# The feed-forward layers' first product by Strassen's seven block products, and their second product in four phases

## The chip, the cores and the metric

The kernel runs on one core of a Trainium2 chip. The metric is the time of one execution on the device, in microseconds; less is better.

## What is computed

A two-layer encoder on 512 tokens of width 1024, in float32. Each layer has a half-step SwiGLU feed-forward (FFN), a mixer of three token-mixing groups, and a second half-step FFN, so there are four FFNs. Around each sub-layer stand an RMS norm, a shift and scale, and a gate, which come from the conditioning vector c by a matrix product (adaLN). What matters here, from the reference:

```python
def swiglu(h, w_in, w_out):
    gate, up = jnp.split(h @ w_in, 2, axis=-1)
    return (jax.nn.silu(gate) * up) @ w_out
...
        h = modulate(rms_norm(x), sh1, sc1)
        x = x + 0.5 * g1[:, None, :] * swiglu(h, w_ff1_in[l], w_ff1_out[l])
```

w_in is 1024 x 5632 and w_out 2816 x 1024: in tiles of 128, w_in gives 22 tiles of gate columns and 22 of up columns, each with 8 tiles along the 1024 rows.

## The kernel before, in words

Activations lie feature by token: a tile is 128 features by 512 tokens. Each product is made of three float32r matmuls (`mm3`, L213 to L220): every float32 operand is split into a high part, a rounded copy by ScalarE (ACT), and a low part, the difference by VectorE (DVE) (`split`, L162 to L165). So the weights of one tile column, 128x1024, go by DMA into a `raw` tile (three buffers), by a cast into `wh` and by a subtraction into `wl` (two buffers each), in `weights` (L167 to L174).

`ffn` (L464 on) runs in two halves of 11 column pairs. For a pair j the gate product `pg` and the up product `pu` are 8 x 3 matmuls of 512 tokens each, so 48 per pair; then ScalarE takes SiLU of `pg`, VectorE multiplies by `pu` (L489), and the result is split into `ah` and `al`. After 11 pairs the second product runs: for each of 8 output tiles m, 33 matmuls into `po`, and VectorE adds gate times `po` to the residual x (`update_x`, L398). In the second half the last two output tiles are done in `tail`, in two token halves of 256 columns, so that the next norm can start on the first half.

The first FFN of layer 0 gets its first four pairs from `start` (L432 on), which streams the normed input row tile by row tile into eight PSUM banks (`pst`). The other FFNs take their first one or two pairs in `norm_first`, beside the norm.

The adaLN product is background work: `ada` (L294 to L301) loads a 128x1024 piece of its matrix and reduces it on VectorE in one instruction. There are 144 pieces; `bg_step` is called after each weight load in an FFN and issues one piece (or a piece of the rotary tables). GpSimd (POOL) adds two shifted copies in the mixer (`shift`, L707) and is idle in the FFNs.

The order on each engine is made by the framework's scheduler from the program's order and its priorities; the kernel's own means are the buffer counts of its pools and where `bg_step` stands. In names below, PE is TensorE and SP the queue that issues the DMAs.

Of the kernel before, what the change touches and what calls it, by code (L numbers as in the profile page):

```python
# [1508 lines left out]
```

## Time and profile before

| what | value |
|---|---|
| median of 3 runs | 2333.05 us (2330.82 to 2336.97) |
| span of the profiled execution | 2329.9 us |
| TensorE (PE) busy | 97% of the span |
| VectorE (DVE) busy | 56% |
| ScalarE (ACT) busy | 40% |
| GpSimd (POOL) busy | 1% |
| mean granted TensorE clock | 0.995 |

The span runs from the first to the last instruction of one profiled execution; the page gives no other time for that execution, and the median of the runs lies 3.1 us above its span. Busy PE time is read with care, because the ends of matmuls are modelled and they overlap: the distance from one start to the next is what a matmul costs.

### The profile page before, as it was taken

To read this page: it belongs to the slowest core of one execution; us is meant where nothing else is said; L and a number is where in the kernel's file an instruction comes from. 1 tells how busy PE (TensorE), PEld (TensorE's weight loads), DVE (VectorE), ACT (ScalarE), POOL (GpSimd) and SP (SyncE) were. 2 spreads that over 40 slices of the span, in tenths; PEclk is the share of its full clock that TensorE was granted. 3 is DMA by queue.
4 is the path that set the end of the run, shared out by engine and by line. 5 is a ranking of instruction groups with operands and counts; after the bars stand their busy time and mean duration, and the time that the engine had idled before them with its cause. 6 is when DMAs were issued, how large, how long until landed. Compare 5 with 4: busy or idle time off the path is not lost.

```text
span 2329.9 us, 33848 instructions
## 1 busy us (share of the span) xinstructions
PE 2269.9 (97%) x14006; PEld 1804.1 (77%) x14006; DVE 1299.0 (56%) x2113; ACT 932.1 (40%) x1473; POOL 32.2 (1%) x48
## 2 busy tenths in 40 slices
PE   6999999999999999999999999999999999999998
PEld 5888888677655788888888888887776568888887
DVE  7656865469555754333455655445785566333334
ACT  3322344533656533223433223454445564322232
POOL 0000000200000000000000000011000000000000
PEclk9999999999999999999999999999999999999999
DMA  7555553212100343332435665322220012223322
GB/s 294 195 204 189 189 200 105 73 55 73 36 18 8 125 153 138 108 100 91 144 110 195 214 219 193 115 73 73 63 57 24 10 35 89 84 90 107 97 89 86
DMA packets 83770, 263.45 MB, mean 113 GB/s; under 512 B 10272, under 2 KB 13600, under 8 KB 83616
## 3 DMA queue, kind: packets, MB, share of 16 engines
q1 hardware_dynamic: 82896, 259.69, 33.7%
q8 instruction: 109, 1.79, 0.3%
q10 hardware_dynamic: 720, 1.61, 0.2%
q14 instruction: 45, 0.37, 0.0%
HBM read 257.07 MB, written 2.10 MB: 111 GB/s over the span
## 4 chain that ended last, share of the span: by engine, by line
PE 88%; DVE 6%; ACT 3%; DMA 2%; issue 1%; POOL 0%; SPq 0%; DVEq 0%; ACTq 0%
PE po L218 7%; PE po L219 7%; PE po L220 7%; PE pu L219 6%; PE pg L219 6%; PE pu L220 6%; PE pg L220 6%; PE pg L218 6%; PE pu L218 6%; PE pz L622 3%; PE pz L623 2%; PE pz L624 2%; PE psc L1328 2%; PE pmo L1364 1%; PE pgram L895 1%; PE ppt L1351 1%
## 5 line engine op out<-in xcount | busy, mean ns | idle before, releaser
L164 ACT CAST wh<-raw 128x1024 fp32r<-128x1024 f32 (+1 forms) x346 | 330.7, 956 | 986.4 <-PE pu L219 264.7
L165 DVE TENSOR_TENSOR wl<-raw,wh 128x1024 fp32r<-128x1024 f32 (+1 forms) x346 | 381.4, 1102 | 378.1 <-ACT wh L164 370.3
L218 PE MATMUL pu<-hh,wh 128*128 128x512 f32 x632 | 245.9, 389 | 0.0
L219 PE MATMUL pu<-hl,wh 128*128 128x512 f32 x632 | 245.9, 389 | 0.0
L219 PE MATMUL pg<-hl,wh 128*128 128x512 f32 x632 | 245.9, 389 | 0.0
L218 PE MATMUL pg<-hh,wh 128*128 128x512 f32 x632 | 245.9, 389 | 0.0
L220 PE MATMUL pu<-hh,wl 128*128 128x512 f32 x632 | 245.8, 389 | 0.0
L220 PE MATMUL pg<-hh,wl 128*128 128x512 f32 x632 | 245.8, 389 | 0.0
L218 PE MATMUL po<-ah,wh 128*128 128x512 f32 x616 | 239.6, 389 | 0.0
L219 PE MATMUL po<-al,wh 128*128 128x512 f32 x616 | 239.6, 389 | 0.0
L220 PE MATMUL po<-ah,wl 128*128 128x512 f32 x616 | 239.6, 389 | 0.0
L301 DVE SCALAR_TENSOR_TENSOR ada<-ada,cb 128x1024 f32<-128x1024 f32 x144 | 175.6, 1220 | 44.3 <-DMA ada<-in_wada_dram 43.9
L489 DVE TENSOR_TENSOR silu<-silu,pu 128x512 f32<-128x512 f32 x79 | 54.3, 688 | 205.1 <-PE pu L220 205.1
L219 PEld LDWEIGHTS pg<-hl,wh 128*128 128x128 f32 x632 | 118.7, 188 | 24.6
L218 PEld LDWEIGHTS pg<-hh,wh 128*128 128x128 f32 x632 | 118.6, 188 | 24.7
L218 PEld LDWEIGHTS pu<-hh,wh 128*128 128x128 f32 x632 | 118.7, 188 | 24.6
L219 PEld LDWEIGHTS pu<-hl,wh 128*128 128x128 f32 x632 | 118.6, 188 | 24.6
L220 PEld LDWEIGHTS pu<-hh,wl 128*128 128x128 f32 x632 | 118.7, 188 | 24.5
L220 PEld LDWEIGHTS pg<-hh,wl 128*128 128x128 f32 x632 | 118.7, 188 | 24.5
L218 PEld LDWEIGHTS po<-ah,wh 128*128 128x128 f32 x616 | 115.7, 188 | 24.0
L219 PEld LDWEIGHTS po<-al,wh 128*128 128x128 f32 x616 | 115.7, 188 | 24.0
L220 PEld LDWEIGHTS po<-ah,wl 128*128 128x128 f32 x616 | 115.6, 188 | 23.9
(396 smaller groups left out, 3899.3 us busy)
## 6 DMA issues: line engine op xcount, KB each, us to landing
ada<-in_wada_dram SPq DMA_DIRECT2D x144, 512.0 KB, 4.4
raw<-in_wff2i_dram SPq DMA_DIRECT2D x88, 512.0 KB, 3.5
raw<-in_wff1i_dram SPq DMA_DIRECT2D x80, 512.0 KB, 3.5
raw<-in_win_dram SPq DMA_DIRECT2D x46, 512.0 KB, 3.5
raw<-in_wff1o_dram SPq DMA_DIRECT2D x28, 384.0 KB, 3.1
raw<-in_wff2o_dram SPq DMA_DIRECT2D x28, 384.0 KB, 3.1
raw<-in_wff1o_dram SPq DMA_DIRECT2D x28, 320.0 KB, 3.0
raw<-in_wff2o_dram SPq DMA_DIRECT2D x28, 320.0 KB, 3.0
```

What stands on the lines that cost most here:

```text
L164: nc.scalar.copy(hi, src)
L165: nc.vector.tensor_tensor(lo, src, hi.bitcast(F32), op=ALU.subtract)
L218: nc.tensor.matmul(ps, lhsT=wh[i], rhs=xh, start=first and i == 0, stop=False)
L219: nc.tensor.matmul(ps, lhsT=wh[i], rhs=xl, start=False, stop=False)
L220: nc.tensor.matmul(ps, lhsT=wl[i], rhs=xh, start=False, stop=last and i == n - 1)
L301: return nc.vector.scalar_tensor_tensor(raw, raw, 1.0, box[0], op0=ALU.mult, op1=ALU.mult, accum_out=t[:, i:i + 1])
L489: nc.vector.tensor_tensor(s, s, pu, op=ALU.mult)
L622: nc.tensor.matmul(ps, lhsT=wh[i], rhs=xh, start=i == 0, stop=False)
L623: nc.tensor.matmul(ps, lhsT=wh[i], rhs=xl, start=False, stop=False)
L624: nc.tensor.matmul(ps, lhsT=wl[i], rhs=xh, start=False, stop=i == n - 1)
L895: nc.tensor.matmul(ps[s * 64:s * 64 + 64, g], lhsT=src[hs, cs], rhs=ar[hs, :, cs], start=True, stop=True)
L1328: nc.tensor.matmul(ps, lhsT=Q[hh][:, qb * P:(qb + 1) * P], rhs=K[hh], start=True, stop=True)
```

## The change

In `ffn`, from pair 4 on in the first FFN and from pair 3 on in the others, `gate_up` takes the place of the two `mm3`. The pair is seen as a 2 x 2 block product: the block rows are gate and up, the inner blocks are the two halves of the 1024 features, and the block columns are the two halves of the tokens. Strassen's method (in Winograd's form) makes it from seven block products of 4 x 3 matmuls of 256 tokens: 84 matmuls of 256 for 48 of 512. For them it needs

- sums of the activations, once per FFN (`sums_x`, on VectorE, with ScalarE and VectorE for the splits: tiles t13 and t24, their parts sh and sl);
- four sums of the weights per pair (`sums_w`, on GpSimd, tiles `ws`), split into one shared tile `w8`, beside the split of gate's weights into `wh` and `wl` and of half of up's into `wsh` and `wsl`;
- four sums of the results in PSUM per pair on VectorE (p6 and p1's copy m1, p5, p7, p3, p7 again).

75 of the 88 pairs are converted: 18 in the first FFN, 19 in each of the others. The second product runs in four phases, after 6, 12, 18 and 22 pairs: for each output tile, 18 matmuls (12 in the last phase) and one update of x. In the last phase four output tiles in place of two are left to `tail`. `bg_step` is called four times in converted pairs below 6, once in later ones, and once or twice per output tile.

```diff
@@ -29,6 +29,9 @@
 H = T // 2
 NSLOT = 53
 WB = 2
+PHASES = (6, 6, 6, 4)
+NTAIL = 4
+Q = H
 E1, G1, I0, I1, I2, U1, U2, C1, Y1, F1 = 700, 300, 250, 4, 1500, 800, 800, 500, 800, 4000
 NA, NB, NZ, N1, N2, TM = 2, 4, 2, 4, 2, 1
 
...
+            self.xs.append(xs)
...
+    def sums_x(self, sh, hs):
+        nc = self.nc
+        dsh = self.small(4, "dsh")
+        nc.vector.tensor_tensor(dsh, sh[:, 4:8], sh[:, 0:4], op=ALU.subtract)
+        t1, t2, t3, t4 = [], [], [], []
+        for k in range(4):
+            a, b = self.xs[k], self.xs[k + 4]
+            u, w = self.slot("t13"), self.slot("t24")
+            nc.vector.tensor_tensor(u[:, 0:Q], a[:, Q:T], a[:, 0:Q], op=ALU.subtract)
+            nc.vector.scalar_tensor_tensor(u[:, Q:T], b[:, Q:T], dsh[:, k:k + 1], a[:, Q:T], op0=ALU.add, op1=ALU.subtract)
+            nc.vector.scalar_tensor_tensor(w[:, 0:Q], a[:, 0:Q], sh[:, k:k + 1], u[:, Q:T], op0=ALU.add, op1=ALU.add)
+            nc.vector.scalar_tensor_tensor(w[:, Q:T], w[:, 0:Q], sh[:, k + 4:k + 5], b[:, 0:Q], op0=ALU.subtract, op1=ALU.subtract)
+            for src, x, y in ((u, t1, t3), (w, t2, t4)):
+                hi, lo = self.split2(src)
+                x.append((hi[:, 0:Q], lo[:, 0:Q]))
+                y.append((hi[:, Q:T], lo[:, Q:T]))
+        first = [tuple(t[:, 0:Q] for t in h) for h in hs]
+        return {"b11": first[0:4], "b21": first[4:8], "b22": [tuple(t[:, Q:T] for t in h) for h in hs[4:8]],
+                "t1": t1, "t2": t2, "t3": t3, "t4": t4}
+
+    def sums_w(self, gate, up):
+        nc = self.nc
+        raws = []
+        for src in (gate, up):
+            raw = self.rawp.tile([P, WCH], F32, tag="raw", name=self.nm("raw"))
+            self.last_dma = nc.sync.dma_start(raw, src).ins
+            raws.append(raw)
+        a, b = raws
+        u, w = (self.arp.tile([P, 1024], F32, tag="ar", name=self.nm("ws")) for _ in range(2))
+        with self.tc.high_priority(offset=1000):
+            nc.gpsimd.tensor_tensor(u[:, 0:T], b[:, 0:T], b[:, T:], op=ALU.add)
+            nc.gpsimd.tensor_tensor(u[:, T:], a[:, 0:T], b[:, 0:T], op=ALU.add)
+            nc.gpsimd.tensor_tensor(w[:, 0:T], u[:, 0:T], a[:, 0:T], op=ALU.add)
+            nc.gpsimd.tensor_tensor(w[:, T:], w[:, 0:T], a[:, T:], op=ALU.add)
+            ah = self.whp.tile([P, WCH], F32R, tag="wh", name=self.nm("wh"))
+            al = self.wlp.tile([P, WCH], F32R, tag="wl", name=self.nm("wl"))
+            ch, cl = self.slot("wsh", F32R), self.slot("wsl", F32R)
+            w8 = self.w8
+            self.split(u, w8[:, 0], w8[:, 1])
+            self.split(a, ah, al)
+            self.split(w, w8[:, 2], w8[:, 3])
+            self.split(b[:, T:], ch, cl)
+
...
+    def product(self, ps, w, xs, first=True, last=True):
+        nc = self.nc
+        wh, wl = w
+        n = len(xs)
+        for i in range(n):
+            xh, xl = xs[i]
+            nc.tensor.matmul(ps, lhsT=wh[i], rhs=xh, start=first and i == 0, stop=False, skip_group_check=True)
+            nc.tensor.matmul(ps, lhsT=wh[i], rhs=xl, start=False, stop=False, skip_group_check=True)
+            nc.tensor.matmul(ps, lhsT=wl[i], rhs=xh, start=False, stop=last and i == n - 1, skip_group_check=True)
...
+    def gate_up(self, gate, up, X):
+        nc = self.nc
+        W = self.sums_w(gate, up)
+        bank = lambda pool, s: self.psum(pool, s)[:, 0:Q]
+        tmp, g, y = self.slot("m1"), self.slot("silu"), self.slot("up")
+        m1, u2 = tmp[:, 0:Q], tmp[:, Q:T]
+        p7 = bank(self.pm, "p7")
+        self.product(p7, W["s3"], X["t3"], last=False)
+        p5 = bank(self.pr, "p5")
+        self.product(p5, W["s1"], X["t1"])
+        p1 = bank(self.pm, "p1")
+        self.product(p1, W["a11"], X["b11"], last=False)
+        nc.scalar.copy(m1, p1)
+        p6 = bank(self.pr, "p6")
+        self.product(p6, W["s2"], X["t2"])
+        nc.vector.tensor_tensor(u2, p6, m1, op=ALU.subtract)
+        nc.vector.tensor_tensor(m1, p5, u2, op=ALU.add)
+        nc.vector.tensor_tensor(y[:, Q:T], m1, p7, op=ALU.subtract)
+        self.product(p1, W["a12"], X["b21"], first=False)
+        nc.scalar.activation(g[:, 0:Q], p1, AF.Silu)
+        p3 = bank(self.pr, "p3")
+        self.product(p3, W["s4"], X["b22"])
+        nc.vector.tensor_tensor(g[:, Q:T], p3, m1, op=ALU.subtract)
+        nc.scalar.activation(g[:, Q:T], g[:, Q:T], AF.Silu)
+        self.product(p7, W["a22"], X["t4"], first=False)
+        nc.vector.tensor_tensor(y[:, 0:Q], u2, p7, op=ALU.subtract)
+        nc.vector.tensor_tensor(g, g, y, op=ALU.mult)
+        return g
+
     def ffn(self, l, which, mods, nsc, nxt, hook=None, begun=None):
         nc = self.nc
         sh, g = mods[0], mods[2]
         wi, wo = self.ap[f"wff{which}i"], self.ap[f"wff{which}o"]
-        ws = {6: ([], []), 7: ([], [])}
-        todo = [(m, o, n) for m in (6, 7) for o, n in ((0, 4), (4, 4), (8, 3))]
-        for half in range(2):
+        plain = 4 if begun else 3
+        X = None
+        j = 0
+        for ph, count in enumerate(PHASES):
+            end = ph + 1 == len(PHASES)
             acts = []
-            for j in range(half * 11, half * 11 + 11):
+            for j in range(j, j + count):
                 if j == 0 and not begun:
                     begun = None, [self.psum(p, "pg") for p in ((self.pm, self.pr) * 2)[:len(self.pre)]]
                     hs = self.norm_first(sh, begun[1], self.pre)
                     self.pre = []
                     begun = hs, begun[1]
-                    pg, pu = begun[1][0:2]
-                elif 2 * j < len(begun[1]):
-                    hs, (pg, pu) = begun[0], begun[1][2 * j:2 * j + 2]
+                hs = begun[0]
+                if X is None:
+                    X = self.sums_x(sh, hs)
+                    if hook:
+                        hook()
+                if j >= plain:
+                    if j == plain:
+                        self.w8 = self.inv8.tile([P, 4, 1024], F32R, tag="U", name=self.nm("w8"))
+                    s = self.gate_up(wi[l, j, 0], wi[l, j, 1], X)
+                    if j < 6:
+                        for _ in range(4):
+                            self.bg_step()
+                    else:
+                        self.bg_step()
                 else:
-                    pg, pu = self.psum(self.pm, "pg"), self.psum(self.pr, "pu")
-                    for gu, ps in enumerate((pg, pu)):
-                        hi, lo = (self.cols(w, 8) for w in self.weights(wi[l, j, gu], 1024))
-                        self.mm3(ps, hi, lo, hs)
-                        self.bg_step()
-                if j == 1 and hook:
-                    hook()
-                s = self.slot("silu")
-                nc.scalar.activation(s, pg, AF.Silu)
-                nc.vector.tensor_tensor(s, s, pu, op=ALU.mult)
+                    if 2 * j < len(begun[1]):
+                        pg, pu = begun[1][2 * j:2 * j + 2]
+                    else:
+                        pg, pu = self.psum(self.pm, "pg"), self.psum(self.pr, "pu")
+                        for gu, ps in enumerate((pg, pu)):
+                            hi, lo = (self.cols(w, 8) for w in self.weights(wi[l, j, gu], 1024))
+                            self.mm3(ps, hi, lo, hs)
+                    s = self.slot("silu")
+                    nc.scalar.activation(s, pg, AF.Silu)
+                    nc.vector.tensor_tensor(s, s, pu, op=ALU.mult)
                 ah = self.slot("ah", F32R)
                 al = self.slot("al", F32R)
                 self.split(s, ah, al)
                 acts.append((ah, al))
-            if half == 1:
...
+            j += 1
+            cs = slice((j - count) * P, j * P)
+            if end:
...
                 tw = self.inv8.tile([P, 4, 1024], F32R, tag="U", name=self.nm("tw"))
-            for m in range(KD - 2 * half):
+                ws = []
+            for m in range(KD - NTAIL * end):
                 po = self.psum(self.pa, "po")
-                src = wo[l, m, half]
-                for o, n in ((0, 6), (6, 5)):
-                    hi, lo = self.weights(src[:, o * P:(o + n) * P], n * P)
-                    self.mm3(po, self.cols(hi, n), self.cols(lo, n), acts[o:o + n], first=o == 0, last=o > 0)
+                hi, lo = self.weights(wo[l, m][:, cs], count * P)
+                self.mm3(po, self.cols(hi, count), self.cols(lo, count), acts)
+                for _ in range(1 + m % 2):
                     self.bg_step()
                 self.update_x(m, po, g)
-                if half == 1:
+                if end:
                     self.sq_add(m, nsc)
...
+                    n = count * P
+                    ws.append(self.weights_at(wo[l, KD - NTAIL + m][:, cs], tw[:, m, 0:n], tw[:, m, 512:512 + n]))
 
         def emit(m, po, th):
-            self.mm3(po, *ws[m], [tuple(t[:, th * H:th * H + H] for t in a) for a in acts])
+            self.mm3(po, *ws[m - KD + NTAIL], [tuple(t[:, th * H:th * H + H] for t in a) for a in acts])
 
         if nxt is not None:
             self.prep(nxt, "aaww")
-        self.tail((6, 7), emit, g, nsc)
+        self.tail(range(KD - NTAIL, KD), emit, g, nsc)
...
             self.ffn(l, 1, self.mods(l, 0), self.mods(l, 1)[1], [self.ap["win"][l, i] for i in range(NZ)],
-                     *((lambda: hook(l, range(2, 9)),) if l else (None, begun)))
...
-        a[f"wff{i}o"] = wo.reshape(L, 2, 11, P, KD, P).transpose(0, 4, 1, 3, 2, 5).reshape(L, KD, 2, P, 11 * P)
+        a[f"wff{i}o"] = wo.reshape(L, NFF, P, KD, P).transpose(0, 3, 2, 1, 4).reshape(L, KD, P, NFF * P)
```

Where it moves instructions, the order on an engine before and now:

VectorE in the first FFN, one pair before: lo parts of gate's and up's weights (`wl`), the product with `pu` (`silu`), the lo part of the activation (`al`), and two adaLN pieces (`ada`).

```order
L165 TENSOR_TENSOR wl_159_848<-raw_157_845,wh_158_847 128x1024
L301 SCALAR_TENSOR_TENSOR ada_173_950,mod_11_135<-ada_173_950,cb_9_130 128x1024
L489 TENSOR_TENSOR silu_152_836<-silu_152_836,pu_143_767 128x512
L165 TENSOR_TENSOR wl_163_881<-raw_161_878,wh_162_880 128x1024
L165 TENSOR_TENSOR al_154_840<-silu_152_836,ah_153_839 128x512
L301 SCALAR_TENSOR_TENSOR ada_177_983,mod_11_135<-ada_177_983,cb_9_130 128x1024
```

The same engine and FFN now, one converted pair in the middle of a phase (n is the pair of m1_428; wl_463 and the second w8 belong to pair n+2, the first w8 and wsl_446 to pair n+1):

```order
L545 TENSOR_TENSOR m1_428_2482<-p6_434_2525,m1_428_2482 128x256
L546 TENSOR_TENSOR m1_428_2482<-p5_432_2498,m1_428_2482 128x256
L547 TENSOR_TENSOR up_430_2484<-m1_428_2482,p7_431_2485 128x256
L168 TENSOR_TENSOR wl_463_2731<-raw_458_2720,wh_462_2730 128x1024
L552 TENSOR_TENSOR silu_429_2483<-p3_435_2554,m1_428_2482 128x256
L168 TENSOR_TENSOR w8_128_599<-ws_442_2595,w8_128_599 128x1024
L555 TENSOR_TENSOR up_430_2484<-m1_428_2482,p7_431_2485 128x256
L307 SCALAR_TENSOR_TENSOR ada_474_2843,mod_11_135<-ada_474_2843,cb_9_130 128x1024
L556 TENSOR_TENSOR silu_429_2483<-silu_429_2483,up_430_2484 128x512
L168 TENSOR_TENSOR w8_128_599<-ws_460_2724,w8_128_599 128x1024
L168 TENSOR_TENSOR al_438_2587<-silu_429_2483,ah_437_2586 128x512
L168 TENSOR_TENSOR wsl_446_2603<-raw_440_2592,wsh_445_2602 128x512
```

Six instructions have become twelve, five of them of 256 columns with an operand in PSUM; one adaLN piece stands where two stood.

VectorE in `start`, behind the last scaled tile of the first norm. Before:

```order
L453 SCALAR_TENSOR_TENSOR xs_88_483<-x_95,mod_11_135,rb_18_151 128x512
L450 TENSOR_SCALAR mod_11_135<-mod_11_135,bada_12_136 128x1
L456 SCALAR_TENSOR_TENSOR hl_90_486<-xs_88_483,mod_11_135,hh_89_485 128x512
L165 TENSOR_TENSOR wl_79_436<-raw_77_433,wh_78_435 128x1024
L301 SCALAR_TENSOR_TENSOR ada_108_573,mod_11_135<-ada_108_573,cb_9_130 128x1024
```

Now (the first of four groups of sums; the others follow between weights and adaLN pieces):

```order
L461 SCALAR_TENSOR_TENSOR xs_88_483<-x_95,mod_11_135,rb_18_151 128x512
L457 TENSOR_SCALAR mod_11_135<-mod_11_135,bada_12_136 128x1
L473 TENSOR_TENSOR dsh_91_513<-mod_11_135 128x4
L464 SCALAR_TENSOR_TENSOR hl_90_486<-xs_88_483,mod_11_135,hh_89_485 128x512
L478 TENSOR_TENSOR t13_92_515<-xs_32_175 128x256
L168 TENSOR_TENSOR wl_79_436<-raw_77_433,wh_78_435 128x1024
L479 SCALAR_TENSOR_TENSOR t13_92_515<-xs_64_351,dsh_91_513,xs_32_175 128x256
L480 SCALAR_TENSOR_TENSOR t24_93_516<-xs_32_175,mod_11_135,t13_92_515 128x256
L481 SCALAR_TENSOR_TENSOR t24_93_516<-t24_93_516,mod_11_135,xs_64_351 128x256
L168 TENSOR_TENSOR sl_95_522<-t13_92_515,sh_94_521 128x512
L168 TENSOR_TENSOR sl_97_526<-t24_93_516,sh_96_525 128x512
```

The sums wait for dsh, and so for the last adaLN piece of the norm. The converted pairs begin right behind the eighth row tile, with no plain pair between.

## Rows read from the trace of the kernel before

**Rows 1.** The page's first part, and its row of PE's granted clock in 40 slices

```profile
PE 2269.9 (97%) x14006; PEld 1804.1 (77%) x14006; DVE 1299.0 (56%) x2113; ACT 932.1 (40%) x1473; POOL 32.2 (1%) x48
...
PEclk9999999999999999999999999999999999999999
```

**Rows 2.** Busy time by stretch: four FFNs, and one mixer (second row)

```profile
core 0: us, PE busy (x) PEld busy (x) DVE busy (x) ACT busy (x) POOL busy (x), PEclk, DMA share, GB/s
73.40:387.60 314.20, 314.20 (x1454) 263.10 (x1453) 205.66 (x321) 108.75 (x152) 0.00 (x0) 1.00 0.56 191
387.60:806.00 418.40, 402.26 (x3541) 285.00 (x3540) 267.61 (x483) 221.91 (x392) 16.00 (x22) 1.00 0.17 53
806.00:1176.00 370.00, 368.11 (x1797) 312.25 (x1798) 161.03 (x232) 118.31 (x170) 0.00 (x0) 1.00 0.36 117
1176.00:1541.00 365.00, 364.02 (x1716) 306.65 (x1714) 206.65 (x318) 122.81 (x175) 0.00 (x0) 1.00 0.51 176
...
1957.00:2322.00 365.00, 363.62 (x1764) 307.97 (x1763) 133.70 (x184) 110.18 (x158) 0.00 (x0) 1.00 0.28 87
```

**Rows 3.** PE by time, 512-column to 256-column products (start us, us)

```profile
365.77 0.39 PE L218 MATMUL po<-ah,wh 128*128 128x512 f32 x1
...
370.53 0.28 PE L218 MATMUL po<-ah,tw 128*128 128x256 f32 x1
...
374.48 0.28 PE L218 MATMUL po<-ah,tw 128*128 128x256 f32 x1
```

**Rows 4.** DVE by time, four instructions back to back

```profile
71.05 1.23 DVE L165 TENSOR_TENSOR wl<-raw,wh 128x1024 fp32r<-128x1024 f32 x1 [0.54 <-ACT wh L164]
72.19 0.69 DVE L165 TENSOR_TENSOR al<-silu,ah 128x512 fp32r<-128x512 f32 x1
72.79 0.68 DVE L489 TENSOR_TENSOR silu<-silu,pst 128x512 f32<-128x512 f32 x1
73.39 1.22 DVE L301 SCALAR_TENSOR_TENSOR ada<-ada,cb 128x1024 f32<-128x1024 f32 x1
```

**Rows 5.** One line (ns min/median/max), then groups by form (busy us, mean ns)

```profile
L411 DVE TENSOR_TENSOR xs<-xs,psb x80: 399/414/422, 383.6 to 1969.1; 128x256 f32<-128x256 f32 x80
...
L164 ACT CAST wh<-raw 128x1024 fp32r<-128x1024 f32 x218 | 229.5, 1053 | 686.0 <-PE pg L219 248.9 <-PE pu L219 232.5 <-issue 87.6
...
L165 DVE TENSOR_TENSOR wl<-raw,wh 128x768 fp32r<-128x768 f32 x72 | 68.9, 957 | 115.0 <-ACT wh L164 114.6
L398 DVE SCALAR_TENSOR_TENSOR x<-po,mod,x 128x512 f32<-128x512 f32 x84 | 62.5, 749 | 67.4 <-PE po L220 56.3 <-PE po L624 10.6
...
L164 ACT CAST ah<-silu 128x512 fp32r<-128x512 f32 x88 | 54.6, 621 | 18.2 <-DVE silu L489 18.2
```

**Rows 6.** POOL and DVE by time, mixer of layer 0: adds alone, and beside DVE

```profile
402.60 1.04 POOL L707 TENSOR_TENSOR zsum<-zc 128x510 f32<-128x510 f32 x1 [402.16 <-ACT zc L704]
403.84 1.04 POOL L707 TENSOR_TENSOR zsum<-zc 128x510 f32<-128x510 f32 x1
403.93 2.33 DVE L709 SCALAR_TENSOR_TENSOR za<-zsum,muh,za 128x512 f32<-128x512 f32 x2 [3.84 <-POOL zsum L708]
...
408.38 1.23 DVE L165 TENSOR_TENSOR wl<-raw,wh 128x1024 fp32r<-128x1024 f32 x1 [2.12 <-ACT wh L164]
408.91 1.60 POOL L707 TENSOR_TENSOR zsum<-zc 128x510 f32<-128x510 f32 x1 [3.44 <-ACT zc L704]
```

**Rows 7.** The line of the DVE instruction that stands beside the adds

```profile
L709 DVE SCALAR_TENSOR_TENSOR za<-zsum,muh,za x18: 746/751/1499, 403.9 to 1605.5; 128x512 f32<-128x512 f32 x18
```

**Rows 8.** DMA issues: KB each, median us from issue to landing

```profile
ada<-in_wada_dram SPq DMA_DIRECT2D x144, 512.0 KB, 4.4
raw<-in_wff1i_dram SPq DMA_DIRECT2D x80, 512.0 KB, 3.5
```

**Rows 9.** DVE at the end of the first norm, and PE's first plain pair behind it

```profile
53.97 0.75 DVE L456 SCALAR_TENSOR_TENSOR hl<-xs,mod,hh 128x512 fp32r<-128x512 f32 x1 [0.79 <-ACT hh L455]
...
L218 PE MATMUL pg<-hh,wh x632: 389/389/396, 69.9 to 2251.4; 128*128 128x512 f32 x158
```

More of the change, by code (lines that the diff above doesn't have):

```diff
@@ L292, in mod_tiles, with ada @@
         self.mod_t[l] = (t, b)
-    def ada(self, l, i, box):
+    def ada(self, l, i, box, first=False):
         nc = self.nc
         t = self.mod_t[l][0]
-        raw = self.big("ada") if i % 3 == 2 else self.arp.tile([P, 1024], F32, tag="ar", name=self.nm("ada"))
+        if first and i % 3 != 2:
+            raw = self.arp.tile([P, 1024], F32, tag="ar", name=self.nm("ada"))
+        else:
+            raw = self.big("ada")
         dma = nc.sync.dma_start(raw, self.ap["wada"][l, i])
@@ L446, in start @@
         hs = []
+        self.xs = []
         for k in range(KD):
             for j in (8 + k, k):
-                self.ada(0, j, box)
+                self.ada(0, j, box, True)
                 nc.vector.tensor_scalar(t[:, j:j + 1], t[:, j:j + 1], b[:, j:j + 1], float(j >= 8), op0=ALU.add, op1=ALU.add)
@@ new lines, in sums_w, with half @@
+    def sums_w(self, gate, up):
[20 more added lines that the diff above has]
+            self.split(b[:, T:], ch, cl)
+        def half(hi, lo, i):
+            return self.cols(hi, 4, i * T), self.cols(lo, 4, i * T)
+        return {"a11": half(ah, al, 0), "a12": half(ah, al, 1), "a22": (self.cols(ch, 4), self.cols(cl, 4)),
+                "s1": half(w8[:, 0], w8[:, 1], 0), "s3": half(w8[:, 0], w8[:, 1], 1),
+                "s2": half(w8[:, 2], w8[:, 3], 0), "s4": half(w8[:, 2], w8[:, 3], 1)}
@@ L499, in ffn @@
                 tw = self.inv8.tile([P, 4, 1024], F32R, tag="U", name=self.nm("tw"))
-            for m in range(KD - 2 * half):
+                ws = []
+            for m in range(KD - NTAIL * end):
                 po = self.psum(self.pa, "po")
-                src = wo[l, m, half]
-                for o, n in ((0, 6), (6, 5)):
-                    hi, lo = self.weights(src[:, o * P:(o + n) * P], n * P)
-                    self.mm3(po, self.cols(hi, n), self.cols(lo, n), acts[o:o + n], first=o == 0, last=o > 0)
+                hi, lo = self.weights(wo[l, m][:, cs], count * P)
+                self.mm3(po, self.cols(hi, count), self.cols(lo, count), acts)
+                for _ in range(1 + m % 2):
                     self.bg_step()
                 self.update_x(m, po, g)
-                if half == 1:
+                if end:
                     self.sq_add(m, nsc)
-                    mm, o, n = todo.pop(0)
-                    src = wo[l, mm, 1][:, o * P:(o + n) * P]
-                    if o < 8:
-                        cs = slice(o * P, (o + n) * P)
-                        w = self.weights_at(src, tw[:, (mm - 6) * 2, cs], tw[:, (mm - 6) * 2 + 1, cs])
-                    else:
-                        w = self.weights_slot(src, n * P)
-                    for lst, t in zip(ws[mm], w):
-                        lst.extend(t)
+                    n = count * P
+                    ws.append(self.weights_at(wo[l, KD - NTAIL + m][:, cs], tw[:, m, 0:n], tw[:, m, 512:512 + n]))
         def emit(m, po, th):
-            self.mm3(po, *ws[m], [tuple(t[:, th * H:th * H + H] for t in a) for a in acts])
+            self.mm3(po, *ws[m - KD + NTAIL], [tuple(t[:, th * H:th * H + H] for t in a) for a in acts])
         if nxt is not None:
             self.prep(nxt, "aaww")
-        self.tail((6, 7), emit, g, nsc)
+        self.tail(range(KD - NTAIL, KD), emit, g, nsc)
     def tail(self, ms, emit, g, nsc):
@@ L1400, in run @@
             self.ffn(l, 1, self.mods(l, 0), self.mods(l, 1)[1], [self.ap["win"][l, i] for i in range(NZ)],
-                     *((lambda: hook(l, range(2, 9)),) if l else (None, begun)))
+                     *((lambda: hook(l, range(3, 9)),) if l else (None, begun)))
             self.bg_flush()
@@ L1406, in run @@
             self.ffn(l, 2, self.mods(l, 2), self.fg if last else self.mods(l + 1, 0)[1],
-                     *((None,) if last else ([self.ap["wff1i"][l + 1, i // 2, i % 2] for i in range(N2)], lambda: hook(l + 1, (0, 1)))))
+                     *((None,) if last else ([self.ap["wff1i"][l + 1, i // 2, i % 2] for i in range(N2)], lambda: hook(l + 1, (0, 1, 2)))))
         self.final()
```

1 line of the change is left out of this document (added).

## The prediction

> **What bounds the kernel now.** I read the page's shares first: PE is busy for 97% of the span at full granted clock, DVE for 56%, POOL for 1% [rows 1]. Then the stretches: in the FFNs after the first norm PE is busy for all but 0 to 2 us of each, so they are PE's columns and nothing else, while DVE differs widely: 206 of 314 us in the first FFN, 161 of 370, 207 of 365 and 134 of 365 us in the others [rows 2]. The difference is mostly the adaLN pieces, which lie in the first and third FFN and the start of the second. So a change that takes columns from PE and gives work to DVE and POOL must be costed on all three.
>
> **What PE saves.** From 365.77 to 370.53 us stand 21 matmuls of 512 columns, 0.2267 us each; from 370.53 to 374.48 us 33 of 256 columns, 0.1197 us each, every one with its own weights [rows 3]. A pair was 48 x 0.2267 = 10.88 us and is 84 x 0.1197 = 10.05 us: 0.83 us less, 62 us for 75 pairs. Seven eighths would be 102 us; the rest goes because two short matmuls take 0.239 us and a long one 0.227, which is about 13 ns for each matmul beside its columns. The Trainium skill ("TensorE: Matmul & The Clock Gate", section "Wait — 56ns, not 53.3ns?") has a fixed cost of about 2.5 ns there; by it the two pairs would be 10.36 and 9.17 us and the saving 89 us. The rows measure this kernel's own instructions, so they decide.
>
> **What DVE and POOL get.** Back to back, a 1024-column instruction takes 1.14 us of DVE and a 512-column one 0.60 us; adaLN's 1.14 [rows 4]. For 256 columns with a PSUM operand I take 0.41 us [rows 5]. A plain pair is 2 x 1.14 + 2 x 0.60 = 3.5 us of DVE. A converted pair is 3 x 1.14 (wl and two of w8) + 3 x 0.60 (wsl, al, product) + 5 x 0.41 = 7.3 us, with one adaLN piece 8.4 us. That alone would fit into 10.05 us.
>
> It doesn't fit with POOL. An add of two 512-column operands is 1.04 us when DVE rests. Beside a wl of DVE (from 408.38 to 409.61 us) the add that began at 408.91 us ended 0.90 us behind wl's end. The other way, a DVE instruction of 0.75 us that began at 403.93 us, under an add that ran to 404.88 us, took 1.50 us [rows 6, 7]. So a POOL add and a DVE instruction with two SBUF operands take turns, whole instructions at a time, and an add holds DVE for 0.90 us. Four adds per pair make 3.6 us: 10.9 us of turns in a pair, 12.0 us with adaLN, less what runs beside the five PSUM instructions (2.05 us), which have one SBUF operand. I assume that those don't take turns; no row shows it.
>
> Where do the adds fall? The three `raw` buffers say: b of pair n+2 overwrites that of pair n, so its load starts when `wsl` of pair n is done. It lands 3.5 to 4.4 us later [rows 8]; then POOL adds one behind the other.
>
> With adaLN, from the end of wsl (0), by the order above: three of 256 columns to 1.23, wl 2.37, next 2.78, w8 3.92, next 4.33. With a landing at 4.4: adaLN 5.47 (first add waits, to 6.37), product 6.97, second add 7.87. Now ACT's cast of the first sums, 1.05 us [rows 5], to 8.92 (third add meanwhile), w8 10.06, fourth add 10.96, al 11.56, wsl 12.16. With a landing at 3.5 the same walk ends at 11.6. I take 11.8: **0.9 us more** than before for a pair, bounds 10.05 and 13 (later landing). There are 17 such full pairs: +15 us.
>
> Without adaLN the second w8 comes behind wsl. The same walk with 4.4 us ends in turn at 9.56 and 10.95 us, 10.3 on average, just over PE's 10.05. I take 10.4, bounds 10.05 and 10.9: 23 pairs, -11 us.
>
> The last two pairs of a phase prepare nothing or little for a next pair, and DVE has 4 to 9 us there: 30 pairs at PE's rate or slightly over, -0.75 each, -22 us. Five pairs right behind the norms carry three or four adaLN pieces beside full sums: 7.3 + 3.5 x 1.14 + 3.6, less 2, is 13 us: +10 us. First product together: **-8 us** (bounds -62 and +70).
>
> The Trainium skill ("GPSIMD Engine Reference", section 3.1) has a two-input add on GpSimd at about 2.6 cycles per element, 1.96 times VectorE's time for it; from 0.60 to 0.69 us that would be 1.18 to 1.35 us, where the row has 1.04. By the page the 17 pairs would lose 10 to 21 us more. The row is of the same operation and width, so it decides.
>
> **Second product.** Matmuls and weight loads are the same. In six of the sixteen phases 11 to 13 adaLN pieces (or the rotary tables) stand beside it: 8 updates of 0.67 + 8 wl of 0.88 (their means less 0.08 of overlap [rows 5]) + 12 x 1.14 + the splits for the next two pairs 6.3 = 32 us of DVE, and eight adds, 7.2 us, of which 5.4 can hide beside the updates. PE needs 8 x 18 x 0.2267 = 32.6 us. I take +2.5 us each, +15 us (bounds 0 and 48).
>
> **The first FFN's start.** The last lo part of the norm was issued at 53.97 us, and PE came to its first plain pair at 69.9 us [rows 9]. All four groups of sums now stand in between: 16 of 0.41 + 8 x 0.60 = 11.4 us, with five weight lo parts and two w8 (8.0), and four adaLN pieces (4.6) before the last sum that p7 needs: 53.97 + 22 to 24 = 76 to 78 us. p7 wants it at 69.9 + 10 x 0.12 = 71 us. **+6 us** (bounds 0 and 8). The other FFNs have one or two plain pairs (11 to 22 us) behind the norm, which hide it.
>
> **Phase ends and last phases.** A phase's first output tile needs the last pair's al behind 15 matmuls, 3.4 us; the way there (0.41 + 0.60 + cast 0.62 [rows 5] + 0.60, with hand-overs 2.7 us) hides. In a last phase it is 9 matmuls, 2.0 us: 0.7 us open, four times, +3 us. The last phase itself is 22 us of PE where 18 to 20 of DVE now stand, and two loads per 2.7 us: +1.5 us each, +6 us (bounds 0 and 16). The three residual passes more per FFN lie on DVE alone.
>
> **Sum:** -8 + 15 + 6 + 3 + 6 = +22 us, 2352 us for the profiled span of 2329.9 us; the median of the runs is 3.1 us higher, so **2355 us**. A check by stretches: in the first FFN DVE's 206 us get 18 x 3.8 + 13 (sums) + 12 (updates) = 299 us, and the adds 65 us, of which up to 62 can hide; PE would need 314 - 15 = 299 us. So this FFN stands between even with PE and 20% over it; the last one (134 + 97 + 68 = 299 against 349) is under in the mean.
>
> **The rivals.**
>
> 1. *PE keeps the bound.* If loads land early enough, or the adds mostly find DVE at PSUM instructions or waiting, all pairs run at 10.05 us: -62, with start 6, ends 9 and 5 for the adaLN phases, is -42: 2291 us. It decides if an adaLN pair stays under 10.1 us. For it: DVE's own work is 8.4 us. Against: the walk finds POOL idle while the PSUM instructions run, since b has not landed. 15%.
> 2. *The turns cost half.* Adds slip into DVE's waits; adaLN pairs come out at 10.9 us, their second-product phases even. -62 + 17 x 0.85 + 10 (the five heavy pairs) + 6 (start) + 9 (ends) = -23: 2310 us. It decides if an add holds DVE for less than 0.5 us on average. For it: five of a converted pair's eleven DVE instructions read PSUM and may leave POOL free. Against: in both rows an add's whole length is waited for [rows 6, 7]. 15%.
> 3. *Loads fall behind.* a, b and an adaLN piece are asked for within about 1 us, 1.5 MB; alone behind one other transfer a piece already takes 4.4 us. If b lands at 6 us, adaLN pairs become 13.5 and the others 11.5: +45 and +14 in place of +15 and -11, with the rest about +77: 2410 us. 15%.
> 4. *The change doesn't do what it says.* The order has the 84 matmuls of 256 per pair, and the four adds on GpSimd; nothing is left for this rival.
>
> The forecast has 55%. About 0.3% (7 us) is what a measurement of this kernel can tell from no change. Forecast's own range is 2325 to 2385 us. The range for 8 in 10 reaches to rival 2 and most of the way to rival 3: **2305 to 2400 us**. Faster by over 0.3%: rivals 1 and 2 and a little of the forecast's lower end, 0.31. Within: 0.13. Slower: 0.56.
>
> **What would show it.** Right: PE's distance from p7's first start to the next pair's, 11 to 12 us in pairs with an adaLN piece, 10.1 to 10.6 without; PE waiting in the table of waits for DVE's w8, m1 or up; adds of 1.6 us or more on POOL, and w8 or al of DVE longer than 1.23 and 0.69 us; a gap of some 6 us in p7 near 71 us; DVE near 75% of the span, POOL near 17%. Wrong: adds that stay at 1.04 us beside DVE, or pairs at 10.05 us in the first FFN (rival 1); loads of raw above 5 us (rival 3); a time below 2325 us.

## The result, and the profile after

The change takes **2563.7 us** (median of 4 runs, 2557.1 to 2565.6) where the kernel before takes 2334.9 us (4 runs, 2330.8 to 2337.0): ratio 1.098, interval 1.0955 to 1.1005, 229 us more. The forecast was 2355 us, range 2305 to 2400. The profiled execution took 2564.2 us, its span 2562.4. Beside the experiments below, the kernel before took 2331 to 2332 us.

The page's first part and the clock row of the change, which answer to [rows 1]:

```profile
PE 2306.8 (90%) x16634; PEld 1928.9 (75%) x16634; DVE 1855.8 (72%) x2810; ACT 1100.8 (43%) x1815; POOL 585.0 (23%) x348
...
PEclk9899899999999989999999999999999999999999
```

PE was idle for 60 us of the span before (2329.9 - 2269.9) and is idle for 256 now. Its busy time rose by 37 us though the matmuls have fewer columns. The same matmuls are busy for 2237.8 us in the run without adds, so the rise comes with the adds. The stages, from PE's first matmul of one to that of the next (us; the first entry counts from the span's start; the last three columns are experiments told below, "phases alone" the second run of that name):

| stage | before | change | adds on VectorE | no adds | phases alone |
|---|---|---|---|---|---|
| start and first FFN | 387.7 | 484.6 | 441.1 | 412.1 | 392.6 |
| mixer, layer 0 | 418.2 | 422.0 | 422.3 | 421.9 | 422.8 |
| FFNs 2 and 3 | 731.0 | 839.7 | 769.3 | 731.2 | 751.6 |
| mixer, layer 1 | 418.4 | 418.5 | 417.5 | 417.2 | 416.3 |
| last FFN | 374.6 | 397.6 | 372.9 | 363.1 | 376.1 |

By stretch, the FFNs of the change in the columns of [rows 2]:

```profile
70.30:484.60 414.30, 334.44 (x2099) 304.50 (x2099) 341.00 (x478) 148.39 (x233) 127.86 (x68) 0.92 0.45 149
...
906.60:1314.30 407.70, 371.32 (x2433) 337.51 (x2433) 299.24 (x406) 156.06 (x247) 138.47 (x76) 0.98 0.33 110
1314.30:1746.30 432.00, 376.22 (x2384) 340.64 (x2384) 337.83 (x474) 167.83 (x264) 141.02 (x76) 0.96 0.42 140
...
2164.80:2562.40 397.60, 365.74 (x2442) 333.14 (x2442) 275.23 (x372) 152.79 (x245) 139.19 (x76) 0.99 0.26 83
```

No engine is full: PE 81 to 92% of a stretch, DVE 69 to 82%. Where work is late and no engine is full, a ring is the first thing to look for: steps of which each waits for the one before, and the first again for the last. One turn, a pair without adaLN in the last FFN, on POOL, then on DVE:

```profile
2412.24 2.13 POOL L500 TENSOR_TENSOR ws<-raw 128x512 f32<-128x512 f32 x1 [4.74 <-DMA raw<-in_wff2i_dram]
2414.34 2.26 POOL L501 TENSOR_TENSOR ws<-raw,raw 128x512 f32<-128x512 f32 x1
2416.55 1.74 POOL L502 TENSOR_TENSOR ws<-ws,raw 128x512 f32<-128x512 f32 x1
2418.37 1.60 POOL L503 TENSOR_TENSOR ws<-ws,raw 128x512 f32<-128x512 f32 x1
2424.69 2.13 POOL L500 TENSOR_TENSOR ws<-raw 128x512 f32<-128x512 f32 x1 [4.72 <-DMA raw<-in_wff2i_dram]
```

```profile
2411.99 1.23 DVE L168 TENSOR_TENSOR wl<-raw,wh 128x1024 fp32r<-128x1024 f32 x1 [1.56 <-ACT wh L167]
2413.13 0.42 DVE L552 TENSOR_TENSOR silu<-p,m 128x256 f32<-128x256 f32 x1
2413.47 1.99 DVE L168 TENSOR_TENSOR w<-ws,w 128x1024 fp32r<-128x1024 f32 x1
2415.38 0.41 DVE L555 TENSOR_TENSOR up<-m,p 128x256 f32<-128x256 f32 x1
2415.89 1.25 DVE L556 TENSOR_TENSOR silu<-silu,up 128x512 f32<-128x512 f32 x1
2417.83 1.02 DVE L168 TENSOR_TENSOR al<-silu,ah 128x512 fp32r<-128x512 f32 x1 [0.69 <-ACT ah L167]
2418.77 1.75 DVE L168 TENSOR_TENSOR wsl<-raw,wsh 128x512 fp32r<-128x512 f32 x1
```

Read the ends in turn. b lands at 2412.24; wl ends at 2413.22; the first add 1.15 us behind it, at 2414.37; w8 1.09 behind that; the second add 1.14 behind w8; the product 0.54; the third add 1.15; al 0.56; the fourth add 1.12, at 2419.97; wsl 0.55, at 2420.52. The fourth add frees the buffer of the next a, which is asked for at 2420.00; that wsl frees the buffer of the next b, which is asked for at 2420.55 and lands by 2424.69, 4.17 us behind wsl. So wl too comes with the load: ACT's cast of a waits for it, and wl for the cast.

```profile
2423.36 1.05 ACT L167 CAST wh<-raw 128x1024 fp32r<-128x1024 f32 x1 [3.83 <-DMA raw<-in_wff2i_dram]
...
2424.44 1.23 DVE L168 TENSOR_TENSOR wl<-raw,wh 128x1024 fp32r<-128x1024 f32 x1 [1.54 <-ACT wh L167]
```

One turn is 12.45 us, and PE's pairs stand some 12.5 us apart. The PSUM instruction of 0.42 us in the midst holds up nobody. With an adaLN piece the line holds that piece and a second w8 as well:

```profile
313.38 2.00 DVE L307 SCALAR_TENSOR_TENSOR ada<-ada,cb 128x1024 f32<-128x1024 f32 x1
...
315.30 1.77 DVE L556 TENSOR_TENSOR silu<-silu,up 128x512 f32<-128x512 f32 x1
317.63 1.65 DVE L168 TENSOR_TENSOR w<-ws,w 128x1024 fp32r<-128x1024 f32 x1 [0.56 <-ACT w L167]
319.20 1.76 DVE L168 TENSOR_TENSOR al<-silu,ah 128x512 fp32r<-128x512 f32 x1
320.89 0.68 DVE L168 TENSOR_TENSOR wsl<-raw,wsh 128x512 fp32r<-128x512 f32 x1
```

Every instruction there but wsl stands under an add, the adaLN piece (1.22 us when alone) too. From the landing of this b at 311.96 us to that of the next at 326.08 us it is 14.1 us. Behind the first phases, 23 pairs hold one or two pieces (the pair with the rotary tables left out). Sixteen of them took 14.1 us on average; the other seven took 15.9 to 19.1 us. In those VectorE stood 2.0 to 4.2 us at a piece whose load had not landed, and the PSUM instructions behind it, for which PE waits, stood with it:

```profile
218.08 0.41 DVE L545 TENSOR_TENSOR m<-p,m 128x256 f32<-128x256 f32 x1
220.54 1.23 DVE L307 SCALAR_TENSOR_TENSOR ada<-ada,cb 128x1024 f32<-128x1024 f32 x1 [2.05 <-DMA ada<-in_wada_dram]
...
221.69 0.42 DVE L546 TENSOR_TENSOR m<-p,m 128x256 f32<-128x256 f32 x1
```

PE's table of waits shows the ring from its side (us in total, times, longest):

```profile
PE p L526 <- ACT m L542: 36.3, 33, 7.0
PE p L526 <- DVE up L555: 30.7, 25, 6.2
PE p L526 <- DVE up L547: 23.4, 39, 2.2
PE p L528 <- DVE w L168: 20.5, 16, 3.7
PE p L526 <- ACT silu L598: 17.1, 1, 17.1
```

Before, the largest of PE's waits in the FFNs, outside the norms, was this:

```profile
PE po L218 <- DVE x L398: 6.0, 5, 2.0
```

The last of the change's five waits is the start. PE, ACT and POOL, then two of the sums' 256-column instructions on DVE:

```profile
87.42 0.58 PE L526 MATMUL p<-sh,w 128*128 128x256 f32 x1 [17.14 <-ACT silu L598]
...
84.84 0.62 ACT L167 CAST sh<-t 128x512 fp32r<-128x512 f32 x1 [2.46 <-DVE t L481]
85.48 1.28 ACT L598 ACT_TABLE_LOAD   x1
...
77.81 2.24 POOL L502 TENSOR_TENSOR ws<-ws,raw 128x512 f32<-128x512 f32 x1
...
78.85 1.48 DVE L478 TENSOR_TENSOR t<-xs 128x256 f32<-128x256 f32 x1
80.25 1.48 DVE L479 SCALAR_TENSOR_TENSOR t<-xs,dsh,xs 128x256 f32<-128x256 f32 x1
```

And the clock. In these windows the eighth entry is the granted clock: 0.59 in the wait of 17.1 us, 0.65 in the 4.6 us behind it, and 0.50, which is 1.2 GHz, from 98 to 104 us, behind another wait of 3.3 us. There 26 matmuls in 5.83 us are 0.224 us each instead of 0.120:

```profile
70.30:87.40 17.10, 0.00 (x0) 0.00 (x0) 15.80 (x20) 5.28 (x7) 6.48 (x4) 0.59 0.54 167
87.40:92.00 4.60, 4.58 (x26) 4.58 (x27) 4.18 (x7) 1.39 (x3) 0.00 (x0) 0.65 0.52 161
98.00:104.00 6.00, 5.83 (x26) 5.79 (x27) 4.54 (x10) 3.48 (x6) 0.00 (x0) 0.50 0.00 0
```

### The profile page after: what moved, and what is told of

Read it like the earlier page. It is cut to its first block, busy times and chain, and to the rows that moved or that the text cites. A ratio compares the mean times of both kernels' runs of the same rounds, so it can differ in the third digit from the quotient of the medians.

```text
span 2562.4 us, 40948 instructions
## 1 busy us (share of the span) xinstructions
PE 2306.8 (90%) x16634; PEld 1928.9 (75%) x16634; DVE 1855.8 (72%) x2810; ACT 1100.8 (43%) x1815; POOL 585.0 (23%) x348
## 4 chain that ended last, share of the span: by engine, by line
PE 44%; DVE 21%; DMA 13%; POOL 8%; issue 7%; ACT 6%; SPq 0%; ACTq 0%; DVEq 0%; POOLq 0%
DMA ada<-in_wada_dram 5%; DVE wl L168 5%; DMA raw<-in_wff2i_dram 4%; PE p L526 3%; PE p L528 3%; PE p L527 3%; POOL ws L501 3%; DMA raw<-in_wff1i_dram 3%; PE po L221 3%; DVE w L168 3%; PE po L222 3%; POOL ws L503 3%; PE pz L727 3%; PE po L223 3%; POOL ws L502 2%
## 5 line engine op out<-in xcount | busy, mean ns | idle before, releaser
L167 ACT CAST wh<-raw 128x1024 fp32r<-128x1024 f32 (+2 forms) x271 | 252.1, 935 | 613.7 <-PE po L222 207.3
L500 POOL TENSOR_TENSOR ws<-raw 128x512 f32<-128x512 f32 x75 | 118.2, 1576 | 1724.4 <-PE pg L717 751.6
L168 DVE TENSOR_TENSOR wl<-raw,wh 128x1024 fp32r<-128x1024 f32 (+2 forms) x271 | 315.7, 1166 | 133.3 <-ACT wh L167 125.2
L526 PE MATMUL p<-sh,w 128*128 128x256 f32 x900 | 265.6, 295 | 43.5 <-ACT silu L598 17.1
L528 PE MATMUL p<-sh,w 128*128 128x256 f32 x900 | 263.0, 293 | 20.5 <-DVE w L168 20.5
L168 DVE TENSOR_TENSOR w<-ws,w 128x1024 fp32r<-128x1024 f32 x150 | 240.2, 1602 | 47.5 <-ACT w L167 47.1
L527 PE MATMUL p<-sl,w 128*128 128x256 f32 x900 | 261.9, 291 | 0.0
L526 PE MATMUL p<-hh,wh 128*128 128x256 f32 x600 | 182.0, 303 | 69.0 <-ACT m L542 36.3
L307 DVE SCALAR_TENSOR_TENSOR ada<-ada,cb 128x1024 f32<-128x1024 f32 x144 | 199.4, 1387 | 56.0 <-DMA ada<-in_wada_dram 55.9
L526 PEld LDWEIGHTS p<-sh,w 128*128 128x128 f32 x900 | 180.3, 200 | 51.5 <-ACT silu L549 22.4
L528 PEld LDWEIGHTS p<-sh,w 128*128 128x128 f32 x900 | 180.0, 200 | 23.7 <-DVE w L168 23.7
L528 PE MATMUL p<-hh,wl 128*128 128x256 f32 x600 | 176.0, 293 | 17.0 <-DVE wl L168 17.0
L527 PEld LDWEIGHTS p<-sl,w 128*128 128x128 f32 x900 | 180.7, 201 | 0.6
L527 PE MATMUL p<-hl,wh 128*128 128x256 f32 x600 | 174.2, 290 | 0.0
```

The source lines that it names most:

```text
L167: nc.scalar.copy(hi, src)
L168: nc.vector.tensor_tensor(lo, src, hi.bitcast(F32), op=ALU.subtract)
L307: return nc.vector.scalar_tensor_tensor(raw, raw, 1.0, box[0], op0=ALU.mult, op1=ALU.mult, accum_out=t[:, i:i + 1])
L500: nc.gpsimd.tensor_tensor(u[:, 0:T], b[:, 0:T], b[:, T:], op=ALU.add)
L526: nc.tensor.matmul(ps, lhsT=wh[i], rhs=xh, start=first and i == 0, stop=False, skip_group_check=True)
L527: nc.tensor.matmul(ps, lhsT=wh[i], rhs=xl, start=False, stop=False, skip_group_check=True)
```

## The experiments

The theory after this reading (A): the ring of load, four adds and five VectorE instructions sets the pairs. Rivals: VectorE's work alone (B), or the loads alone (C).

**Four raw buffers.** `raw` bufs 3 -> 4, NSLOT 53 -> 51.

> Four raw buffers instead of three (two slots fewer to make room); nothing else. Theory A (a ring: the load of a pair's weights waits for the last add and the wsl of an earlier pair, the first add waits for that load, and the four adds go in turns with five VectorE instructions): the load of 4.2 us leaves the ring, a pair without adaLN goes from 12.46 us to 10.1 to 10.5, one with adaLN from 14.5 to 11 to 11.5; time 2430 to 2475 us, and GpSimd no longer waits 4.7 us for raw in each pair, while its adds stay at 1.6 to 2.3 us. Theory B (VectorE's own work, adaLN included, is too much for a pair, loads or not): 2545 to 2570 us. Theory C (the loads alone are the bound, the turns cost nothing): all pairs at 10.05 to 10.2 us, under 2420 us.

2530.1 us, between the cases. Pairs fell as A said: the six of a phase without adaLN from 71 to 76 us down to 62.4 to 62.7 (10.4 each), those with adaLN to 66 to 69 (11.0 to 11.5 each, the phase with the rotary tables apart). But second products rose from 32.7 us to 38 to 43 us. VectorE near the end of one:

```profile
1107.68 1.78 DVE L168 TENSOR_TENSOR wsl<-raw,wsh 128x512 fp32r<-128x512 f32 x1
1111.73 1.23 DVE L168 TENSOR_TENSOR w<-ws,w 128x1024 fp32r<-128x1024 f32 x1 [2.27 <-ACT w L167]
1115.22 1.28 DVE L168 TENSOR_TENSOR w<-ws,w 128x1024 fp32r<-128x1024 f32 x1 [2.27 <-ACT w L167]
1116.42 2.02 DVE L168 TENSOR_TENSOR wl<-raw,wh 128x768 fp32r<-128x768 f32 x1
1118.36 1.40 DVE L404 SCALAR_TENSOR_TENSOR x<-po,mod,x 128x512 f32<-128x512 f32 x2
```

With a buffer more, the next phase's splits come earlier in VectorE's order; there they wait for ACT's casts and so for the adds, and two due residual updates wait behind them, and for these PE:

```profile
1119.25 0.77 PE L221 MATMUL po<-ah,wh 128*128 128x512 f32 x1 [4.98 <-DVE x L404]
```

**The same, with those splits held back**, by an order dependency on the last `wl` of the second product:

```diff
+            if self.hold is not None:
+                for lo in los:
+                    self.after(lo, self.hold)
```

> Four raw buffers as in the run before, and the lo parts of the sums that a phase prepares for the next are kept behind the last lo part of the second product's weights on VectorE. Theory A (ring and turns; the earlier load had pulled these lo parts ahead of the due residual updates, and that gave the gain back): pairs as in the run with four buffers (10.4 us, 11.0 to 11.5 with adaLN), second products of 32.7 to 35 us instead of 38 to 43: 2435 to 2465 us. Rival (the work of VectorE and GpSimd has to be paid somewhere, so the first pairs of the phases get it): 2500 to 2535 us.

2495.0 us, between the cases and close to the rival's: second products mostly 34 us, pairs without adaLN 10.8 in the steady part; the last FFN took 377.6 us, 20 less than in the change. Pairs with adaLN stayed at 11 to 15 us. So both cases hold in part: the load was in the ring, and something stays when it has gone. That these are the turns is argued here, not shown.

**The adds on VectorE.** `nc.gpsimd.tensor_tensor` -> `nc.vector.tensor_tensor`, four times.

> The four adds of the weights' sums on VectorE instead of GpSimd, raw buffers still three. Theory A: no turns are left; an add is 0.60 us rather than 1.1 us plus a wait, VectorE has 9.7 us per pair (10.9 with adaLN), the ring shrinks to some 10.5 us, 11 to 11.5 with adaLN: 2400 to 2460 us. Theory B (VectorE's work is the bound): each of the 75 pairs gets up to 2.4 us longer, 2600 us or more. Theory C (loads): 2540 to 2570 us.

2424.6 us, ratio 1.0389 (1.0374 to 1.0405): VectorE gets 300 instructions of 0.60 us back to back more, and the kernel is 139 us faster. Each takes its own time again (the group's mean: 1.60 us in the change, 1.39 and 1.39 the next two):

```profile
L168 DVE TENSOR_TENSOR w<-ws,w 128x1024 fp32r<-128x1024 f32 x150 | 183.4, 1223 | 16.4 <-ACT w L167 16.1
L307 DVE SCALAR_TENSOR_TENSOR ada<-ada,cb 128x1024 f32<-128x1024 f32 x144 | 175.6, 1222 | 32.8 <-DMA ada<-in_wada_dram 32.4
L168 DVE TENSOR_TENSOR wl<-raw,wh 128x1024 fp32r<-128x1024 f32 x143 | 174.7, 1222 | 53.9 <-ACT wh L167 52.8
```

B falls. C falls as well, since the loads are unchanged. It doesn't tell the turns from GpSimd's slower add, since both go with the move.

**Both.** Adds on VectorE and four buffers.

> The four adds on VectorE, and four raw buffers. If with the adds on VectorE the load is still in the ring: pairs go from 10.7 us to 10.2 to 10.4 us, 2395 to 2412 us. If VectorE's own order is the bound there: 2418 to 2430 us.

2422.4 us (two runs, 2414 and 2431; the profile is of the faster), in time as without the fourth buffer, so that VectorE's case holds by the total. The pairs say less clearly so: the first five of a phase of six without adaLN took 51.8 us instead of 52.9 to 57.4, which is 10.4 each and in the other case's range, while the last FFN's way to its second phase got 10 us longer (113.8 instead of 104.0). With the adds on VectorE the load is worth little, but it isn't shown to be out of the ring.

**No adds.** The sums' tiles go; `split(b, ...)` and `split(a, ...)` take the place of `split(u, ...)` and `split(w, ...)`.

> The four adds are left out: the weights themselves are split where the sums were, so that products are not those of the reference; loads, splits, matmuls and adaLN stay. Theory A: VectorE 7.3 us (8.4 with adaLN) and no turns, pairs at 10.1 us nearly everywhere; what is left over before is the start of the first FFN (10 us or more) and the stalls behind the rotary tables: 2310 to 2370 us. Theory B: over 2450 us. Theory C (loads): over 2500 us.

2347.3 us (a single run): all that hangs on the adds is 216 us. Of these 77 come with the adds wherever they are (2424.6 - 2347.3), 139 with GpSimd. Pairs without adaLN mostly took 10.1 us, the price of their columns.

**One operand instead of two on GpSimd.**

```diff
-            nc.gpsimd.tensor_tensor(u[:, 0:T], b[:, 0:T], b[:, T:], op=ALU.add)
+            nc.gpsimd.tensor_scalar(u[:, 0:T], b[:, T:], 1.0, None, op0=ALU.add)
```

> The four GpSimd instructions stay, with the same outputs, waits and loads, but each reads one tile and adds a constant instead of adding two tiles; the products are not those of the reference. Theory A (an add on GpSimd and a VectorE instruction with two operands in SBUF take turns; that is what makes the ring long): if one operand frees the other engine, the four are under 1.1 us each with no wait on VectorE, wl, w8 and al stay at 1.22, 1.22 and 0.69 us, pairs at 10.1 to 11 us: 2340 to 2400 us. Rival (the ring is long because of the load and of four instructions in a row on GpSimd, turns or not, or any GpSimd instruction takes turns): 2480 to 2565 us; the VectorE durations tell the two apart.

2515.6 us, on the rival's side, though in part for a reason that neither had: the one-operand instruction is longer, 1.48 us at least against 1.27 for the add.

```profile
2362.67 2.32 POOL L500 TENSOR_SCALAR ws<-raw 128x512 f32<-128x512 f32 x1 [5.00 <-DMA raw<-in_wff2i_dram]
2364.96 1.58 POOL L501 TENSOR_SCALAR ws<-raw 128x512 f32<-128x512 f32 x1
2366.51 1.50 POOL L502 TENSOR_SCALAR ws<-raw 128x512 f32<-128x512 f32 x1
2367.97 1.68 POOL L503 TENSOR_SCALAR ws<-raw 128x512 f32<-128x512 f32 x1
```

VectorE is hardly held any more (the w8 of the sums 1.29 us on average, the product 0.77 instead of 1.06), but four in a row are 7.0 us and the loads 5.0: 12.0 us a turn. GpSimd's chain closes the ring with the load even where VectorE isn't held; how the 139 us divide between the two stays open. An estimate, from rows of the change: four adds that nothing holds are 4 x 1.28 = 5.1 us, and with the 4.72 us before the first of them a turn would be 9.8 us, under PE's 10.08. By it such adds would not set a pair without adaLN; no run has two-operand adds on GpSimd that nothing holds.

**Phases alone.** First `plain = NFF`:

> All 22 pairs of each FFN by the plain product, the second product still in phases of 6, 6, 6 and 4 tiles (the sums of the activations are not removed from the code but their result is not read). Theory A: the four phases cost little by themselves, 2335 to 2365 us, the sums of the activations included. Rival: the phases (adaLN pieces and residual passes beside six-pair phases) carry a good part of the 229 us: over 2400 us.

2383.7 us, between the cases: the plain branch issues no adaLN pieces, so these ran in a heap at the FFNs' ends (the first FFN's last second product took 42.6 us). Then with as many pieces as the change issues, and without the sums of the activations:

> The plain product for all 22 pairs, four phases, no sums of the activations, and as many adaLN pieces per pair and tile as the change issues (the run before this one issued none in the pairs). The weights keep the layout of the change. Theory A: the four phases cost little by themselves and the 52 us of the former run were adaLN pieces left to the ends of the FFNs: 2333 to 2350 us. Rival (the phases themselves cost): 2370 us or more.

2360.4 us, ratio 1.0116 (1.0095 to 1.0136): above theory A's range, below the rival's; that last second product took 26.4 us. The phases and their adaLN timetable cost 28 us, 21 of it in FFNs 2 and 3. There four pieces per pair crowd into the first phase, and its second product took 40.3 and 35.7 us where PE needs 32.6.

**adaLN moved** out of the pairs from the seventh on; `1 + m % 2` -> `2 + m % 2` pieces per tile of the second product.

> The change with no adaLN piece in the pairs from the seventh on; each tile of the second product issues one more instead. Theory A: an adaLN piece is one more link of some 2.2 us in the ring, so the twenty pairs with one go from 14.5 us to 12.5 us, while the second product has VectorE free: 2505 to 2535 us. Rival (it is the amount of VectorE's work that costs, wherever it lies): 2555 to 2575 us.

2554.8 us, at the edge of the rival's range. The pairs that lost their piece did mostly take 11 to 14 us; but twenty pieces were more than a second product takes, and the rest piled up at the next phase's first pair (21.6 us for the first FFN's seventh pair, 15.0 in the change).

**The start.** `plain = 6` in the first FFN, with the pairs' adaLN pieces.

> In the first FFN the pairs 4 and 5 by the plain product too, with the same adaLN pieces; everything else as in the change. Theory: the 17 us in which TensorE waits for the sums of the activations at the start go, since two plain pairs (21.8 us) stand in front of the first converted one, which by then has its sums; 2540 to 2552 us. Rival (VectorE is behind by as much and gives it back in the first phase's end or the second product): 2555 to 2570 us.

2549.7 us, 14 less: as the theory said.

**Filler.** Twelve matmuls more per pair, before the product with a12.

```diff
+        junk = bank(self.pa, "junk")
+        self.product(junk, W["s2"], X["t2"])
```

> Twelve more matmuls of 256 columns in each of the 75 converted pairs, into a bank that nobody reads: 1.44 us of TensorE each at full clock, 108 us in all. Theory A (the ring through the loads, GpSimd and VectorE sets the pairs, TensorE has some 2.4 us of waits in each): only the last pairs of phases and the few others at 10.1 us get longer, 25 to 50 us more, 2585 to 2615 us. Rival (TensorE's own time, with the low clock and the gaps behind its waits, sets the pairs): 95 to 115 us more, 2655 us or more.

2610.8 us: 47 us more for 108 us of columns. PE has the rest to spare, in pairs that wait; so its low clock is for the most part not what sets them.

## Why the prediction was wrong

The sign was right and rests on the right pair of engines; the size was not: +22 us forecast, +229 measured. Term by term:

- **PE's saving** held: with the adds out, pairs without adaLN mostly take 10.1 us.
- **The walk of a pair is the step that failed.** It gave 11.8 us with adaLN and 10.4 without; from one pair's first matmul to the next's, in the phases after the first and without each phase's last pair, the 23 pairs with one or two pieces took 15.2 us on average and 28 without 12.2. Those two kinds lie 98 and 38 us over plain pairs, where "first product together: -8 us" stood for all. Its parts:
  - The add's price. An add ends 1.12 to 1.15 us behind the VectorE instruction, not 0.90, which is 1 us per pair for four. I had priced it with the shortest of eighteen (1.04 us; their median was 1.59, which [rows 7] should have made me look up on POOL's side). The add alone takes 1.27 to 1.30 us here. The estimate that I set aside was nearer: by the Trainium skill ("GPSIMD Engine Reference", section 3.1) it was 1.18 to 1.35.
  - The ring. "Third add meanwhile" hid one add behind ACT's cast, while all four stand in the line. And the walk has wl at 1.2 to 2.4 us behind wsl, as if a were there; but the fourth add asks for a, and wl began 3.9 us behind wsl, with b's landing.
  - adaLN's own loads, which the walk doesn't have: in seven of the 23 pairs VectorE waited for one. (The change also leaves the pieces behind `start` only the three `inv` buffers, where they had the four of `ar` too. No run gives these back; without adds VectorE waited 30.8 us for pieces with the same three, 55.9 in the change.)
  - The pair before the last of a phase. The last two were priced at PE's rate; behind the first phases the last took 10.1 to 11.6 us, the one before it 11.7 to 19.1.
- That **PSUM instructions don't take turns**, which no row had shown, held: 0.41 to 0.42 us beneath adds. Those with two SBUF operands wait for whole adds: the product took 1.25 us in the turn shown, 0.69 in the run with the adds on VectorE. The Trainium skill ("GPSIMD Engine Reference", section "8. Key points") names VectorE instructions with two SBUF inputs as those that contend; the trace agrees for these, by the product's 1.25 us.
- **Loads** of gate's and up's weights took 3.4 us in the median, as forecast, and b landed 4.2 to 4.5 us behind wsl in the turns shown; six of 168 took more than 5 us (5.1 to 5.7). So rival 3, that loads are slow, was at most a small part of it: they were asked for late.
- **The start** was +17 us, not +6. The 22 to 24 us of VectorE work were priced without turns: eight instructions of the stretch take some 8 us more under the adds than their kinds do alone, and p7's bank waits for a silu behind the last cast and a 1.28 us table load on ACT.
- **adaLN second products** were priced at +15 us and took 32 to 35 us each, where PE needs 32.6: next to nothing. The phases with their adaLN timetable cost 28 in all (the second run of phases alone), near the 24 that I had for ends and second products, but not where I put it. The residual passes are two more per FFN, not three as I wrote.
- **Not in the sum at all**: the rotary tables before pair 12 of the first FFN (27.7 us for that pair) and PE's clock. Worked out from the clock's records and the starts of matmuls, some 55 to 60 us of full-rate columns start at half clock, some 10 before; this makes PE's busy time longer. The filler bears on it: PE's own time is not what sets most pairs.
- **The whole, against the phases alone** (span 2359.4, so 203 us to find): some 137 us are the 98 and 38 above, 17 the pair with the rotary tables, 53 the four first phases with the start's 17 among them (I had 16 for their five heavy pairs and the start), and the last pairs of phases give back 5.

No version here beats the kernel before: even the one without adds, which leaves work out, is 0.7% above it by its single run, and the last FFN with adds on VectorE is even with it (372.9 against 374.6 us).

## What to carry to other kernels

Before you hand work to an idle engine, ask whether its instructions take turns with those of the one that it relieves, and if they do, price both as one line, at their median beside each other, not at their shortest alone. Where loads wait for consumers and consumers for loads, write down which step asks for each load, and go round until it repeats: here no engine was above 92% busy, and the ring set the time. And a buffer added to open a ring changes the scheduler's order; look at what it pulled ahead.
